# Low parts of weights by adding DMAs at the stage boundaries of a four-layer network, and a later place in the code for the second layer's modulation

## The chip, the cores and the metric

The kernel runs on 1 core of one Trainium2 chip. The metric is the device time of one execution in microseconds (us); lower is better. A core has five engines that work side by side, each in its own fixed order: TensorE (PE, with its weight loads PEld), VectorE (DVE), ScalarE (ACT), GpSimd (POOL) and SyncE (SP, which here only issues DMAs). ACT and POOL can issue DMAs too.

## What is computed

One sequence of 512 tokens (and 256 context tokens) of width 1024 passes four transformer layers. The first two belong to a diffusion block: differential attention, then neighbourhood attention, each followed by an MLP, with scales and shifts ("modulation") that are made from a condition vector. The last two mix retention and windowed attention and have an MLP too. Cut to the part that the change touches:

```python
h = modulate(rms_norm(x, norm2_g[i]), mod_l[3], mod_l[4])
x = x + mod_l[5] * (jnp.square(jax.nn.relu(h @ w_mlp1[i])) @ w_mlp2[i])      # layers 0 and 1
ff = jnp.square(jax.nn.relu(u @ w_ff1[l])) @ w_ff2[l]                         # layers 2 and 3
mod = jax.nn.silu(c) @ w_mod[i] + b_mod[i]                                    # per layer 0 and 1
```

All in float32. Token counts differ: 512 + 256 columns in layer 0, 512 in layer 1, 528 in layers 2 and 3.

## The kernel before, in words

Activations lie with features on the 128 partitions and tokens in the free dimension. PE multiplies in a faster 32-bit format that keeps fewer bits, so every operand is split: a high part (the value rounded to that format) and a low part (value minus high part). Each product is then three matmuls: high x high, high x low, low x high (`mm3`, line 228).

Every weight tile of 128 x 1024 (512 KB) comes through a ring that `wring` makes: SP loads it into a raw buffer `wr`, ACT copies it to `wh` (the high part), and `parts` computes `wl = wr - wh` by a subtraction (line 250) on POOL, or on DVE where the ring was made with `eng=V`. A ring has a few raw buffers (2 or 3) and 5 to 8 pairs of `wh` and `wl`; a pair comes free when PE has used it, a raw buffer when both readers have.

Stages follow each other: `layer0` (attention), `post(0)` (the output weights `wo`, a norm, the MLP), `layer1`, `post(1)`, then twice `block2` (retention, windowed attention, a mixing product `wmix`, the MLP) with `front` for the first projections of the next one. `mlp` runs over eight blocks c = 0..7 of the hidden width. A block takes four tiles of the first weight and four of the second. In c = 0 and c = 7 the tokens go in two groups one after the other, so that the norm of one group can run while PE works on the other; c = 1..6 take all tokens together, and in all but layer 0 use a scheme with seven instead of eight products, for which `load.sums` adds quarters of the weight tile on POOL. By "boundary" the text means such a c = 0 or c = 7 with the norm, `wo`, `wmix` or `front` beside it.

A norm (`rstd`) squares eight tiles on ACT into `nt`, adds them on DVE into `na`, lets PE sum over the partitions (line 380, tile `n`), takes logarithm and exponential on ACT (`nr`), and then DVE scales (`nt`), ACT writes the high part `bigB` and DVE the low part `bigC`. In an MLP block ACT writes relu into `ms`, DVE squares it (line 884 or 212), ACT makes the high part `hh` and DVE the low part `hl`.

The second layer's modulation (`modulation(1, c)`, six parts) is a chain: SP loads a weight tile `wmg` (one buffer), POOL multiplies it by the condition (line 341, tile `wmu`, one buffer), ACT sums it up.

A scheduler puts the instructions of each engine in order from a simulated time line, so an instruction's place in the code is only its rank; each engine then keeps that order and waits at every instruction until its inputs are there.

Of the kernel before, what the change touches and what calls it, by code (L numbers as in the profile page):

```python
# [10 lines left out]
F32 = mybir.dt.float32  # L11
F32R = mybir.dt.float32r
BF16 = mybir.dt.bfloat16
AF = mybir.ActivationFunctionType
ALU = mybir.AluOpType
# [159 lines left out]
class Program:  # L175
# [59 lines left out]
    def wring(self, *parts, size=1024, low=None, eng=None):  # L235


        ws = [(pl, n) for pl, n, _ in parts for _ in range(n)]
        rs = [(pl, n) for pl, _, n in parts for _ in range(n)]
        aw, ar = count(), count()  # L240

        def raw():
            w, n = rs[next(ar) % len(rs)]
            return self.tl(w, "wr", [128, size], n)

        def parts(r, c, eng):
            w, n = ws[next(aw) % len(ws)]
            h, l = (self.tl(q, tag, [128, size], n, F32R) for q, tag in ((w, "wh"), (low or w, "wl")))
            self.act(h[:, c], r[:, c], AF.Copy)
            eng.tensor_tensor(l[:, c], r[:, c], h[:, c].bitcast(F32), op=ALU.subtract)  # L250
            return h, l

        def load(src, c=slice(0, size)):

            r = raw()
            self.nc.sync.dma_start(r[:, c], src)
            return parts(r, c, eng or self.G)

        def sums(src):

            r, s = raw(), raw()
            self.nc.sync.dma_start(r, src)
            (a11, a12, a22, a21), (s1, s2, s3, s4) = ([t[:, i * 256:i * 256 + 256] for i in range(4)] for t in (r, s))
            for o, a, b, op in ((s1, a21, a22, ALU.add), (s2, s1, a11, ALU.subtract),
                                (s3, a11, a21, ALU.subtract), (s4, a12, s2, ALU.subtract)):
                self.G.tensor_tensor(o, a, b, op=op)
            return parts(r, slice(0, 768), self.G), parts(s, slice(0, 1024), self.V)
        load.sums = sums
        return load
# [171 lines left out]
    def layer0(self):  # L441
        nc, V, T, ap = self.nc, self.V, self.T, self.ap
# [3 lines left out]
        st = ExitStack()  # L446
        with st:
            wp = st.enter_context(self.phase("l0w"))
            load = self.wring((wp, 5, 2), size=768)
            rp = st.enter_context(self.phase("l0r"))  # L450

            def weights(h, u):
# [133 lines left out]
            low = count()  # L586
# [132 lines left out]
    def post(self, i):  # L719
        nc, V, T, ap = self.nc, self.V, self.T, self.ap  # L720
        both = i == 0
        A, B, C = self.Af, self.B, self.C

        if both:
            gs = [(A[:, :, :512], B[:, :, :512], C[:, :, :512], slice(0, 512), 0),
                  (self.af, self.b[:, :, :], self.c[:, :, :], slice(512, 768), 1)]
            joint = gs
        else:
            gs = [(A[:, :, s], B[:, :, s], C[:, :, s], s, 0) for s in (slice(16, 272), slice(272, 528))]
            s = slice(16, 528)  # L730
            joint = [(A[:, :, s], B[:, :, s], C[:, :, s], s, 0)]
        width = 768 if both else 528
        with self.psum(a=(1, 6), n=(1, 2)), self.phase("pw") as wp, self.phase("post") as pl:
            load = self.wring((wp, 8, 2), eng=V) if both else self.wring((self.wp, 5, 2), (wp, 3, 1))
            self.nw, self.nb = (512, 3) if both else (336, 5)
            if not both:
                nc.scalar.dma_start(A[:, :, :16], ap["metaT"])
            for X, H, L, _, j in joint:
                for h in range(EARLY, 8):
                    self.split(H[:, h], L[:, h], X[:, h])  # L740

            cut = [slice(EARLY * 128 if m < EARLY else 0, 1024) for m in range(8)]
            order = (6, 7, 0, 1, 2, 3, 4, 5)
            us = {m: load(ap["wo"][i, m][:, cut[m]], cut[m]) for m in order}
            gate = self.modT[i][:, 2]
            for g, (X, H, L, s, j) in enumerate(gs):
                n = s.stop - s.start
                for m in order:
                    early = m < EARLY
                    o = X[:, m]  # L750
                    if early:
                        xo = o
                    else:
                        xo = self.tl(pl, "ms", [128, width], 2)[:, :512 if j == 0 else 256]
                        nc.scalar.dma_start(xo, (ap["xT"], ap["ctxT"])[j][:, m] if both else self.spill[:, m])
                    p = self.pt("a")[:, :n]
                    wh, wl = us[m]
                    self.mm3([p], [(wh[:, k * 128:(k + 1) * 128], wl[:, k * 128:(k + 1) * 128],
                                    [H[:, k]], [L[:, k]]) for k in range(EARLY if early else 0, 8)])
                    if not both and not early:  # L760
                        xo = xo.rearrange("p (c r) -> p r c", r=8)[:, 4 * g:4 * g + 4]
                        p = p.rearrange("p (r c) -> p r c", r=4)
                        o = o.rearrange("p (r c) -> p r c", r=4)
                    V.scalar_tensor_tensor(o, p, gate[:, m, j:j + 1], xo, op0=ALU.mult, op1=ALU.add)
                self.norm_mod(pl, i, 3, X, n, j, H, L)

            gate5 = self.modT[i][:, 5]

            def fin(m, c, g, p):
                X, j = g[0], g[4]  # L770
                V.scalar_tensor_tensor(X[:, m], p, gate5[:, m, j:j + 1], X[:, m], op0=ALU.mult, op1=ALU.add)  # L771

            def after(g):
                X, H, L, s, j = gs[g]
                if both:
                    self.norm_mod(pl, 1, 0, X, s.stop - s.start, j, H, L)
                else:
                    self.b2_norm(pl, 0, g)
                    if g == 1 and self.stop > 1:
                        self.front(0)  # L780

            if both:
                for c in (1, 0, 2, 3, 4, 5):
                    self.modulation(1, c)
            else:
                self.decays(pl)
            fast = None
            if not both:
                fast = [g[3] for g in gs], [self.split4(t) for t in (self.tl(self.b5, "bigD", [128, 8, 528], 1, F32R), self.F)]
            self.mlp(pl, load, ap["w1"][i], ap["w2"][i], width, (gs, joint, gs), fin, after, fast)  # L790

    def mlp(self, pl, load, w1, w2, width, gs, fin, after, fast=None, before=None):

        V, G, T = self.V, self.G, self.T

        def block(us, j, k):

# [86 lines left out]
        for c in range(8):  # L887
            quick = fast and 0 < c < 7
            if c == 7 and before:
                before()  # L890
            u1 = [(load.sums if quick else load)(w1[c * 4 + j]) for j in range(4)]
            u2 = [load(w2[c * 4 + j]) for j in range(4)]
            hid = [(self.tl(pl, "hh", [128, width], 4, F32R), self.tl(pl, "hl", [128, width], 4, F32R))
                   for j in range(4)]
            parts = [gs[1]] if 0 < c < 7 else [[g] for g in gs[c // 7 * 2]]
            if quick:
                for j in range(0, 4, 2):
                    product7(u1[j:j + 2], hid[j:j + 2])
            for i, part in enumerate(parts):
                if not quick:  # L900
                    for j in range(4):
                        first(u1, j, part, hid[j])
                for m in range(8):
                    second(m, c, u2, part, hid)
                if c == 7:
                    after(i)
            if fast and c == 0:
                sums()


    def layer1(self):
        nc, V, T, G, ap = self.nc, self.V, self.T, self.G, self.ap
        st = ExitStack()
        with st:
            st.enter_context(self.psum(pj=(1, 2), tq=(1, 1), s=(1, 2), n=(1, 2), po=(1, 1)))

            pp, wp, kp, lp, pl = (st.enter_context(self.phase('l1' + n)) for n in 'pwkla')
            load = self.wring((wp, 5, 2), size=768, low=lp)
            half = (slice(0, 64), slice(64, 128))
            hL, hC = (self.B, self.C), (self.b, self.c)  # L920
            self.spill = self.dr.tile([128, 8, 512], F32, name="spill")
# [160 lines left out]
    def front(self, li):  # L1082
# [6 lines left out]
        QG = (slice(q0, EG[0].stop), EG[1])  # L1089
        QJ = EG if li == 0 else (qa,)  # L1090
        half = (slice(0, 64), slice(64, 128))
        load = self.wring((self.wp, 5, 2))

        def mmu(w, gs, hold=()):
            ps = [self.pt("a")[:, :s.stop - s.start] for s in gs]
# [12 lines left out]
        class Rot:  # L1108
# [3 lines left out]
                u.f, u.keys = f, keys  # L1112
                u.groups, u.joint = (EG, EG) if keys else (QG, QJ)

            def start(u):
                u.w = load(ap["wfm"][li, u.f])
                u.raw = self.tl(self.b5, "rr", [128, 528], 2)

            def run(u, gs):
# [51 lines left out]
        class Gate:  # L1171
# [2 lines left out]
            def __init__(u, h):  # L1174
                u.h = h

            def start(u):
                u.w = load(ap["wfm"][li, 8 + u.h])
                u.raw = self.tl(self.b5, "gr", [128, 528], 2)

            def run(u, gs):
# [8 lines left out]
        Gate.groups, Gate.joint = QG, QJ  # L1190
        units = [(("k", 0), Rot(4, True)), (("q", 0), Rot(0, False)), (("g", 0), Gate(0)), (("g", 1), Gate(1))]
        for _, u in units:
            u.start()
            u.run(u.groups[:1])
        self.parts = lows, units, load, mmu, Rot, Gate, score, gate, qa, QG, QJ, half

# [408 lines left out]
```

## Time and profile before

| | |
|---|---|
| median of 3 runs | 3781.81 us (3781.76 to 3787.19) |
| the profiled execution | 3784.63 us |
| its span (first to last instruction) | 3782.8 us |
| mean granted TensorE clock | 0.963 of full speed |
| busy share PE, DVE, ACT, POOL | 92%, 67%, 50%, 48% |

PE is the busiest engine, but the table is an average: in long stretches of the MLPs PE is busy all the time, and at the boundaries it waits for what DVE and ACT make. A change at the boundaries is to be read there.

### The profile page before, as it was taken

To read this page: it belongs to the slowest core of one execution; us is meant where nothing else is said; L and a number is where in the kernel's file an instruction comes from. 1 tells how busy PE (TensorE), PEld (TensorE's weight loads), DVE (VectorE), ACT (ScalarE), POOL (GpSimd) and SP (SyncE) were. 2 spreads that over 40 slices of the span, in tenths; PEclk is the share of its full clock that TensorE was granted. 3 is DMA by queue.
4 is the path that set the end of the run, shared out by engine and by line. 5 is a ranking of instruction groups with operands and counts; after the bars stand their busy time and mean duration, and the time that the engine had idled before them with its cause. 6 is when DMAs were issued, how large, how long until landed. Compare 5 with 4: busy or idle time off the path is not lost.

```text
span 3782.8 us, 58120 instructions
## 1 busy us (share of the span) xinstructions
PE 3484.6 (92%) x22512; PEld 3186.7 (84%) x22512; DVE 2529.1 (67%) x4189; ACT 1887.8 (50%) x3891; POOL 1816.3 (48%) x1218
## 2 busy tenths in 40 slices
PE   6888887999999999899999999979997999988998
PEld 6788876878888998788899999979997888787888
DVE  5778867543335777777677666486667767558766
ACT  5777766432125876533356665443334666544333
POOL 4666654430002655587732332457763233356884
PEclk9999998999999999899999999989999999999999
DMA  5222223432112222223332221323332222242333
GB/s 197 78 73 70 67 95 124 151 117 73 56 56 73 58 61 67 81 84 101 112 100 77 78 73 55 112 74 102 93 127 84 82 88 73 61 133 64 101 95 106
DMA packets 118566, 338.00 MB, mean 89 GB/s; under 512 B 13905, under 2 KB 37330, under 8 KB 118034
## 3 DMA queue, kind: packets, MB, share of 16 engines
q1 hardware_dynamic: 105664, 315.97, 26.8%
q10 hardware_dynamic: 12626, 18.32, 1.6%
q8 instruction: 176, 2.88, 0.3%
q14 instruction: 100, 0.82, 0.1%
HBM read 321.39 MB, written 12.86 MB: 88 GB/s over the span
## 4 chain that ended last, share of the span: by engine, by line
PE 54%; DVE 22%; ACT 7%; issue 6%; DMA 5%; POOL 5%; ACTq 0%; POOLq 0%; SPq 0%; DVEq 0%
PE a L228 40%; PE pj L228 6%; DMA wmg<-in_wmod 3%; DVE ms L884 3%; POOL wmu L341 3%; DVE hl L217 2%; DVE P L649 1%; DVE ms L212 1%; ACT wh L207 1%; DVE na L212 1%; DVE nt L212 1%; POOL wl L250 1%; PE po L1307 1%; DVE bigC L217 1%; ACT qd L207 1%
## 5 line engine op out<-in xcount | busy, mean ns | idle before, releaser
L250 POOL TENSOR_TENSOR wl<-wr,wh 128x1024 fp32r<-128x1024 f32 (+2 forms) x416 | 971.4, 2347 | 1032.5 <-ACT wh L207 913.5
L207 ACT ACTIVATE wh<-wr 128x1024 fp32r<-128x1024 f32 (+3 forms) x560 | 536.9, 972 | 758.9 <-PE a L228 409.4
L228 PE MATMUL a<-bigB,wh 128*128 128x256 f32 (+3 forms) x2140 | 637.0, 315 | 25.8 <-ACT bigB L216 16.3
L228 PE MATMUL a<-bigC,wh 128*128 128x256 f32 (+3 forms) x2140 | 643.7, 315 | 9.6 <-DVE bigC L217 9.6
L228 PE MATMUL a<-bigB,wl 128*128 128x256 f32 (+3 forms) x2140 | 640.0, 314 | 1.4 <-DVE wl L250 1.4
L228 PE MATMUL a<-hl,wh 128*128 128x256 f32 (+2 forms) x1664 | 492.9, 334 | 19.0 <-DVE hl L217 18.6
L228 PE MATMUL a<-hh,wh 128*128 128x256 f32 (+2 forms) x1664 | 465.8, 333 | 36.7 <-ACT hh L216 25.5
L228 PE MATMUL a<-hh,wl 128*128 128x256 f32 (+2 forms) x1664 | 486.8, 331 | 0.0
L341 POOL TENSOR_TENSOR wmu<-wmg,sc 128x1024 f32<-128x1024 f32 x128 | 320.7, 2505 | 271.9 <-DMA wmg<-in_wmod 190.5
L228 PEld LDWEIGHTS a<-bigB,wh 128*128 128x128 f32 x2140 | 395.6, 192 | 53.3 <-ACT bigB L216 18.2
L228 PEld LDWEIGHTS a<-bigC,wh 128*128 128x128 f32 x2140 | 396.5, 191 | 37.4 <-DVE bigC L217 13.9
L228 PEld LDWEIGHTS a<-bigB,wl 128*128 128x128 f32 x2140 | 396.2, 191 | 25.5 <-DVE wl L250 2.1
L228 PEld LDWEIGHTS a<-hh,wh 128*128 128x128 f32 x1664 | 288.3, 193 | 75.2 <-ACT hh L216 30.1
L228 PEld LDWEIGHTS a<-hl,wh 128*128 128x128 f32 x1664 | 296.8, 193 | 61.2 <-DVE hl L217 33.6
L250 DVE TENSOR_TENSOR wl<-wr,wh 128x1024 fp32r<-128x1024 f32 (+1 forms) x144 | 203.9, 1423 | 180.3 <-ACT wh L207 180.3
L228 PEld LDWEIGHTS a<-hh,wl 128*128 128x128 f32 x1664 | 295.8, 193 | 26.5
L228 PE MATMUL a<-bigF,wh 128*128 128x256 f32 (+3 forms) x1024 | 295.1, 294 | 4.1 <-ACT bigF L216 4.1
L217 DVE TENSOR_TENSOR hl<-ms,hh 128x512 fp32r<-128x512 f32 (+4 forms) x160 | 198.7, 1261 | 61.4 <-ACT hh L216 60.6
L228 PEld LDWEIGHTS a<-bigF,wh 128*128 128x128 f32 x1024 | 194.2, 192 | 7.2 <-ACT bigF L216 4.6
L209 ACT ACTIVATE wmu<-wmu 128x1024 f32<-128x1024 f32 x128 | 135.1, 1056 | 118.2 <-POOL wmu L341 117.7
L228 PE MATMUL a<-bigD,wh 128*128 128x256 f32 (+2 forms) x640 | 187.0, 303 | 5.8 <-ACT bigD L216 3.3
L771 DVE SCALAR_TENSOR_TENSOR bigA<-a,modT,bigA 128x512 f32<-128x512 f32 (+1 forms) x144 | 96.2, 687 | 140.3 <-PE a L228 140.2
(350 smaller groups left out, 8711.8 us busy)
## 6 DMA issues: line engine op xcount, KB each, us to landing
wr<-in_w SPq DMA_DIRECT2D x128, 512.0 KB, 3.6
wr<-in_wf SPq DMA_DIRECT2D x128, 512.0 KB, 3.5
wmg<-in_wmod SPq DMA_DIRECT2D x80, 512.0 KB, 3.5
wr<-in_wfm SPq DMA_DIRECT2D x76, 512.0 KB, 3.5
wr<-in_wqkv SPq DMA_DIRECT2D x64, 384.0 KB, 3.3
wm<-in_wmod SPq DMA_DIRECT2D x16, 512.0 KB, 7.5
wr<-in_wv SPq DMA_DIRECT2D x16, 512.0 KB, 3.4
wr<-in_wret SPq DMA_DIRECT2D x16, 512.0 KB, 3.5
```

Source lines behind the costliest of these rows:

```text
L207: self.S.activation(o, i, f, bias=bias, scale=scale)
L209: self.S.activation(o, i, f, bias=bias, scale=scale, accum_out=accum)
L212: self.V.tensor_tensor(o, a, b, op=op)
L217: self.V.tensor_tensor(lo, src, hi.bitcast(F32), op=ALU.subtract)
L228: self.T.matmul(o, w, x, start=(i == 0 and j == 0), stop=(i == n - 1 and j == 2))
L250: eng.tensor_tensor(l[:, c], r[:, c], h[:, c].bitcast(F32), op=ALU.subtract)
L341: self.G.tensor_tensor(u, w, self.sc[:, j], op=ALU.mult)
L649: V.scalar_tensor_tensor(P[0], P[1], cf[:, t:t + 1], P[0], op0=ALU.mult, op1=ALU.add)
L771: V.scalar_tensor_tensor(X[:, m], p, gate5[:, m, j:j + 1], X[:, m], op0=ALU.mult, op1=ALU.add)
L884: V.scalar_tensor_tensor(r[:, s], r[:, s], 0.0, r[:, s], op0=ALU.max, op1=ALU.mult)
L1307: T.matmul(po[g], x[:n, t - 1], y[:, s], start=False, stop=(t == 4 and j == 2))
```

## The change

Where a `load` gets `eng=None`, the low part is now made without a subtraction: ACT writes minus the high part into `wl`, and a DMA issued by POOL adds the weight from DRAM to it (`accum_op=ALU.add`). This path is taken by the `wo` tiles of both `post`s, the `wmix` tiles, all eight tiles of blocks c = 0 and c = 7 of the four MLPs, and the first four units of `front`: 104 tiles, 12 of them of 128 x 256. Of these, 80 were subtractions on POOL and 24 on DVE. Blocks c = 1..6 keep their engine, and so do the attention stages. The call of `modulation(1, c)` moves from ahead of the MLP of layer 0 to behind its blocks 1 to 6.

```diff
-        def parts(r, c, eng):
+        def parts(r, c, eng, src=None):
             self.act(h[:, c], r[:, c], AF.Copy)
-            eng.tensor_tensor(l[:, c], r[:, c], h[:, c].bitcast(F32), op=ALU.subtract)
+            if eng is None:
+                self.act(l[:, c], h[:, c].bitcast(F32), AF.Copy, scale=-1.0)
+                self.G.dma_start(l[:, c], src, accum_op=ALU.add)
+            else:
+                eng.tensor_tensor(l[:, c], r[:, c], h[:, c].bitcast(F32), op=ALU.subtract)
...
-            load = self.wring((wp, 8, 2), eng=V) if both else self.wring((self.wp, 5, 2), (wp, 3, 1))
+            load = self.wring((wp, 8, 2)) if both else self.wring((self.wp, 5, 2), (wp, 3, 1))
...
-            if both:
-                for c in (1, 0, 2, 3, 4, 5):
-                    self.modulation(1, c)
-            else:
+            if not both:
                 self.decays(pl)
...
+            self.mlp(pl, load, ap["w1"][i], ap["w2"][i], width, (gs, joint, gs), fin, after, fast,
+                     beside=(lambda c: self.modulation(1, (1, 0, 2, 3, 4, 5)[c])) if both else None)
...
+        eng = G if fast else V, None
...
-            u1 = [(load.sums if quick else load)(w1[c * 4 + j]) for j in range(4)]
-            u2 = [load(w2[c * 4 + j]) for j in range(4)]
+            if quick:
+                u1 = [load.sums(w1[c * 4 + j]) for j in range(4)]
+            else:
+                u1 = [load(w1[c * 4 + j], eng=eng[c in (0, 7)]) for j in range(4)]
+            u2 = [load(w2[c * 4 + j], eng=eng[c in (0, 7)]) for j in range(4)]
...
+            if beside and 0 < c < 7:
+                beside(c - 1)
```

Three places of the resulting order. First POOL at the start of `post(0)`, where before only the modulation of layer 1 (`wmu`) stood, first before and then after the change:

```order
L341 TENSOR_TENSOR wmu_5792<-wmg_5790,sc 128x1024
L341 TENSOR_TENSOR wmu_5795<-wmg_5790,sc 128x1024
L341 TENSOR_TENSOR wmu_5800<-wmg_5798,sc 128x1024
L341 TENSOR_TENSOR wmu_5803<-wmg_5798,sc 128x1024
L341 TENSOR_TENSOR wmu_5808<-wmg_5806,sc 128x1024
```

```order
L345 TENSOR_TENSOR wmu_7336<-wmg_7334,sc 128x1024
L345 TENSOR_TENSOR wmu_7339<-wmg_7334,sc 128x1024
L252 DMA wl_5317<-in_wo 128x1024
L345 TENSOR_TENSOR wmu_7344<-wmg_7342,sc 128x1024
L252 DMA wl_5324<-in_wo 128x1024
L252 DMA wl_5331<-in_wo 128x256
L252 DMA wl_5338<-in_wo 128x256
L345 TENSOR_TENSOR wmu_7347<-wmg_7342,sc 128x1024
L252 DMA wl_5345<-in_wo 128x256
```

The modulation stands at the same place among POOL's instructions although its call moved: the first adding DMA of `wo` comes behind the sixth `wmu` of the second part, and the second one behind the seventh.

Second, PE at the boundary into the MLP of `block2(0)`: the last products of `wmix` (`bigD`, `bigF` their operands) and the sum `n` of the first token group's norm, before and after:

```order
L228 MATMUL a_25161<-bigD_18834,wl_24659 128x256
L228 MATMUL a_25161<-bigD_18834,wh_24658 128x256
L228 MATMUL a_25161<-bigF,wh_24658 128x256
L228 MATMUL a_25161<-bigD_18834,wl_24659 128x256
L380 MATMUL n_24944<-na_24945,ones 128x272
L228 MATMUL a_25161<-bigD_18834,wh_24658 128x256
L228 MATMUL a_25161<-bigF,wh_24658 128x256
L228 MATMUL a_25161<-bigD_18834,wl_24659 128x256
```

```order
L228 MATMUL a_25247<-bigF,wh_24723 128x256
L228 MATMUL a_25247<-bigD_18886,wl_24724 128x256
L228 MATMUL a_25247<-bigD_18886,wh_24723 128x256
L228 MATMUL a_25247<-bigF,wh_24723 128x256
L384 MATMUL n_25004<-na_25005,ones 128x272
L228 MATMUL a_25247<-bigD_18886,wl_24724 128x256
L228 MATMUL a_25468<-bigB,wh_25406 128x272
L228 MATMUL a_25498<-bigB,wh_25406 128x272
```

Before, `n` stands behind 15 of the 24 matmuls of the last product but one; 33 more of `wmix` follow it, and then the MLP's first product, which takes `bigB`, the result of that norm. Now `n` stands one matmul ahead of that first product, 32 places later than before.

Third, ACT at the same boundary, around the norm of the first token group (`nt` the squares, `nr` its logarithm and exponential, `bigA` copies out of PSUM, `bigB` high parts), before and after:

```order
L207 ACTIVATE wh_25370<-wr_25368 128x1024
L207 ACTIVATE bigA_72<-a_25109 128x256
L207 ACTIVATE nt_24965<-bigA_72 128x272
L207 ACTIVATE wh_25376<-wr_25374 128x1024
L207 ACTIVATE bigA_72<-a_25135 128x256
L207 ACTIVATE nr_24969<-n_24944,eps 128x272
L207 ACTIVATE na_25214<-bigA_72 128x256
L207 ACTIVATE nr_24969<-nr_24969 128x272
```

```order
L207 ACTIVATE wl_25435<-wh_25434 128x1024
L207 ACTIVATE wh_25441<-wr_25439 128x1024
L207 ACTIVATE bigA_72<-a_25195 128x256
L207 ACTIVATE nt_25025<-bigA_72 128x272
L207 ACTIVATE wl_25442<-wh_25441 128x1024
L207 ACTIVATE wh_25448<-wr_25446 128x1024
L207 ACTIVATE bigA_72<-a_25221 128x256
L207 ACTIVATE wl_25449<-wh_25448 128x1024
L207 ACTIVATE wh_25455<-wr_25453 128x1024
L207 ACTIVATE nr_25029<-n_25004,eps 128x272
L207 ACTIVATE na_25274<-bigA_72 128x256
L207 ACTIVATE nr_25029<-nr_25029 128x272
```

The last square now stands one product's copy (`bigA`) later, three `wh` copies and the `wl` negations of the second weight stand ahead of the logarithm, and a fourth negation, which the excerpt's end leaves out, stands between logarithm and exponential (with one more copy out of PSUM).

## Rows read from the trace of the kernel before

**Rows 1.** The page: span, and busy time of each engine.

```profile
span 3782.8 us, 58120 instructions
PE 3484.6 (92%) x22512; PEld 3186.7 (84%) x22512; DVE 2529.1 (67%) x4189; ACT 1887.8 (50%) x3891; POOL 1816.3 (48%) x1218
```

**Rows 2.** Table by stretch: length, busy PE, PEld, DVE, ACT, POOL, clock, DMA, GB/s.

```profile
560.00:670.00 110.00, 82.96 (x370) 65.78 (x371) 84.71 (x97) 64.42 (x117) 46.09 (x20) 0.89 0.40 129
830.00:1120.00 290.00, 290.00 (x1651) 252.61 (x1651) 112.48 (x139) 63.76 (x84) 6.30 (x9) 1.00 0.19 59
1530.00:1670.00 140.00, 120.63 (x811) 113.15 (x812) 111.80 (x172) 63.86 (x127) 98.73 (x74) 0.88 0.28 89
...
2450.00:2610.00 160.00, 138.38 (x1024) 134.34 (x1023) 128.51 (x206) 64.83 (x125) 104.25 (x74) 0.91 0.31 94
...
2790.00:2940.00 150.00, 124.13 (x939) 120.25 (x939) 105.44 (x182) 65.40 (x131) 60.99 (x41) 0.92 0.33 106
3370.00:3500.00 130.00, 105.60 (x754) 98.35 (x753) 110.62 (x181) 54.55 (x114) 82.51 (x60) 0.93 0.29 91
```

**Rows 3.** The page's groups of weight splitting: count, busy us, mean ns, idle before.

```profile
L250 POOL TENSOR_TENSOR wl<-wr,wh 128x1024 fp32r<-128x1024 f32 (+2 forms) x416 | 971.4, 2347 | 1032.5 <-ACT wh L207 913.5
L207 ACT ACTIVATE wh<-wr 128x1024 fp32r<-128x1024 f32 (+3 forms) x560 | 536.9, 972 | 758.9 <-PE a L228 409.4
...
L250 DVE TENSOR_TENSOR wl<-wr,wh 128x1024 fp32r<-128x1024 f32 (+1 forms) x144 | 203.9, 1423 | 180.3 <-ACT wh L207 180.3
```

**Rows 4.** Timeline of DVE, 2449 to 2472 us: start, duration, instruction, count.

```profile
2455.77 0.98 DVE L212 TENSOR_TENSOR na<-na,nt 128x272 f32<-128x272 f32 x2
2457.60 2.11 DVE L212 TENSOR_TENSOR bigA<-nt,xo 128x272 f32<-128x272 f32 x1 [0.86 <-DMA xo<-spill]
...
2460.34 6.01 DVE L212 TENSOR_TENSOR na<-na,nt 128x272 f32<-128x272 f32 x4
...
2471.32 2.41 DVE L217 TENSOR_TENSOR bigC<-nt,bigB 128x272 fp32r<-128x272 f32 x1 [0.31 <-ACT bigB L216]
```

**Rows 5.** Timeline of POOL in the same stretch.

```profile
2456.99 2.43 POOL L250 TENSOR_TENSOR wl<-wr,wh 128x1024 fp32r<-128x1024 f32 x1 [2.15 <-ACT wh L207]
2461.20 4.85 POOL L250 TENSOR_TENSOR wl<-wr,wh 128x1024 fp32r<-128x1024 f32 x2 [1.79 <-ACT wh L207]
```

**Rows 6.** Timelines of PE, then of ACT, at the same boundary.

```profile
2466.40 1.28 PE L380 MATMUL n<-na,ones 128*128 128x272 f32 x2 [7.39 <-DVE na L212]
2473.59 0.67 PE L228 MATMUL a<-bigB,wh 128*128 128x272 f32 x4
...
2470.86 1.70 ACT L216 ACTIVATE bigB<-nt 128x272 fp32r<-128x272 f32 x5
```

**Rows 7.** Waits of PE for `na`, 1530 to 1670, then 3370 to 3500 us: total, times, longest.

```profile
PE n L380 <- DVE na L212: 3.6, 1, 3.6
...
PE n L380 <- DVE na L212: 8.1, 2, 7.2
```

**Rows 8.** Waits of PE, 1900 to 1990 us.

```profile
PE a L228 <- DVE hl L217: 4.4, 2, 3.8
```

**Rows 9.** Waits of PE, 2790 to 2940 us.

```profile
PE n L380 <- DVE na L212: 9.9, 1, 9.9
...
PE a L228 <- DVE bigC L217: 2.7, 2, 2.3
PE a L228 <- DVE hl L217: 2.6, 2, 1.5
```

**Rows 10.** DMA issues of 512 KB, by tile: count, KB each, median us to landing.

```profile
wr<-in_wf SPq DMA_DIRECT2D x128, 512.0 KB, 3.5
...
wm<-in_wmod SPq DMA_DIRECT2D x16, 512.0 KB, 7.5
```

**Rows 11.** Timeline from 566 us: POOL's modulation products, PE's first use of a low part.

```profile
567.30 2.36 POOL L341 TENSOR_TENSOR wmu<-wmg,sc 128x1024 f32<-128x1024 f32 x1 [1.26 <-ACT wmu L209]
570.79 0.79 PE L228 MATMUL a<-bigB,wl 128*128 128x512 f32 x1 [1.35 <-DVE wl L250]
575.82 2.40 POOL L341 TENSOR_TENSOR wmu<-wmg,sc 128x1024 f32<-128x1024 f32 x1 [6.16 <-DMA wmg<-in_wmod]
```

More of the change, by code (lines that the diff above doesn't have):

```diff
@@ L249, in parts, with load @@
             self.act(h[:, c], r[:, c], AF.Copy)
-            eng.tensor_tensor(l[:, c], r[:, c], h[:, c].bitcast(F32), op=ALU.subtract)
+            if eng is None:
[3 more added lines that the diff above has]
+                eng.tensor_tensor(l[:, c], r[:, c], h[:, c].bitcast(F32), op=ALU.subtract)
             return h, l
-        def load(src, c=slice(0, size)):
+        def load(src, c=slice(0, size), eng=eng):
             r = raw()
             self.nc.sync.dma_start(r[:, c], src)
-            return parts(r, c, eng or self.G)
+            return parts(r, c, eng, src)
         def sums(src):
@@ L448, in layer0 @@
             wp = st.enter_context(self.phase("l0w"))
-            load = self.wring((wp, 5, 2), size=768)
+            load = self.wring((wp, 5, 2), size=768, eng=self.G)
             rp = st.enter_context(self.phase("l0r"))
@@ L789, in post, with mlp @@
                 fast = [g[3] for g in gs], [self.split4(t) for t in (self.tl(self.b5, "bigD", [128, 8, 528], 1, F32R), self.F)]
-            self.mlp(pl, load, ap["w1"][i], ap["w2"][i], width, (gs, joint, gs), fin, after, fast)
-    def mlp(self, pl, load, w1, w2, width, gs, fin, after, fast=None, before=None):
+            self.mlp(pl, load, ap["w1"][i], ap["w2"][i], width, (gs, joint, gs), fin, after, fast,
+                     beside=(lambda c: self.modulation(1, (1, 0, 2, 3, 4, 5)[c])) if both else None)
+    def mlp(self, pl, load, w1, w2, width, gs, fin, after, fast=None, before=None, beside=None):
         V, G, T = self.V, self.G, self.T
+        eng = G if fast else V, None
         def block(us, j, k):
@@ L917, in layer1 @@
             pp, wp, kp, lp, pl = (st.enter_context(self.phase('l1' + n)) for n in 'pwkla')
-            load = self.wring((wp, 5, 2), size=768, low=lp)
+            load = self.wring((wp, 5, 2), size=768, low=lp, eng=G)
             half = (slice(0, 64), slice(64, 128))
@@ L1091, in front @@
         half = (slice(0, 64), slice(64, 128))
-        load = self.wring((self.wp, 5, 2))
+        G = self.G
+        load = self.wring((self.wp, 5, 2), eng=G)
         def mmu(w, gs, hold=()):
@@ L1113, in __init__, with start @@
                 u.groups, u.joint = (EG, EG) if keys else (QG, QJ)
-            def start(u):
-                u.w = load(ap["wfm"][li, u.f])
+            def start(u, eng=G):
+                u.w = load(ap["wfm"][li, u.f], eng=eng)
                 u.raw = self.tl(self.b5, "rr", [128, 528], 2)
@@ L1175, in __init__, with start @@
                 u.h = h
-            def start(u):
-                u.w = load(ap["wfm"][li, 8 + u.h])
+            def start(u, eng=G):
+                u.w = load(ap["wfm"][li, 8 + u.h], eng=eng)
                 u.raw = self.tl(self.b5, "gr", [128, 528], 2)
@@ L1192, in front @@
         for _, u in units:
-            u.start()
+            u.start(None)
             u.run(u.groups[:1])
```

## The prediction

> **What bounds the kernel now.** I read the page's busy shares first: PE is busy 92% of the span, some 298 us are left over [rows 1]. A table by stretch says where those lie: between 830 and 1120 us, inside the MLP of layer 0, PE is busy for all of its 290 us at the full clock, while in the stretches at the boundaries it idles 16 to 27 us each and the granted clock falls to 0.88 to 0.93 [rows 2]. There DVE is busy about 80% of the time, and POOL works beside it. So PE bounds the inside of the MLPs, where no edit can win, and the chain through DVE and ACT bounds the boundaries; all that the change does is to be priced at the boundaries.
>
> What lengthens that chain is seen by laying DVE's timeline against POOL's at one boundary. Two adds `na` of 128x272 take 0.98 us while POOL is idle, so 0.49 each; four of them take 6.01 us across two POOL subtractions of 4.85 us in all; one `bigA` of the same size takes 2.11 us where it meets a POOL subtraction of 2.43, and `bigC` takes 2.41 [rows 4, 5]. A DVE operation with two SBUF inputs is thus held until POOL's subtraction ends. On the path into `n` this costs 6.01 - 4x0.49 = 4.0 and 2.11 - 0.49 = 1.6 us, together 5.7, and there PE waits 7.4 us [rows 6]. The same wait is 3.6 and 7.2 us at the two like boundaries [rows 7].
>
> **The change part by part.** It takes 80 subtractions from POOL, 80 x 2.347 = 188 us, and 24 from DVE, 24 x 1.423 = 34 us. It gives ACT 104 negations of up to 0.972 us, at most 101 us [rows 3], 104 DMA issues to POOL, and 92 x 512 KB + 12 x 128 KB = 49.6 MB of weights that are read a second time. In the boundary stretches DMA is busy 0.28 to 0.40 [rows 2].
>
> The trace has no POOL issue of an adding DMA and no landing of one. Issue: from 0 to 2.35 us (the subtraction that it replaces); I take 1, as it moves no data itself. Landing: the two transfers of 512 KB shown take 3.5 and 7.5 us [rows 10]; I take 5, nearer to the weights' 3.5 since the source is a weight too, with more for reading the destination. A low part thus comes 0.97 + 1 + 5 = 7.0 us after its high part, where POOL's came 2.35 after: 4.6 us later, between 2.1 (0 and 3.5) and 8.5 (2.35 and 7.5).
>
> The Trainium skill, "DMA: Bandwidth & Descriptors", section "Anatomy of one DMA", fits a POOL-issued DMA as 2.0 us plus the bytes by 436 GB/s; an estimate from it is 3.2 us for 512 KB, and with that term (d) below would be about half. It speaks of plain transfers, and no run here shows an adding one.
>
> (a) *Three boundaries from `wo` or `wmix` into c = 0* (1530, 2450, 3370 us). At 2450 PE was ready for `n` at 2466.40 - 7.39 = 2459.01. In the new order `n` stands 32 matmuls later; one takes 138.38/1024 = 0.135 us [rows 2], so PE reaches it at 2459.0 + 4.3 = 2463.3. Freed of POOL, `na` is done at 2466.4 - 5.7 = 2460.7; two more ACT operations on the way to the last square (a negation and a `wh` copy, 0.97 each) make it 2462.6. So `n` waits for nothing and runs at 2463.3. But its 33 matmuls of cover have gone ahead of it, and behind it PE now waits for `bigB`. Before, `n` started at 2466.40 and the first of five `bigB` was there at 2470.86 + 0.34 [rows 6], 4.8 us later; with the negation that now stands between logarithm and exponential, 5.8. First product: 2469.1 instead of 2473.59, a gain of 4.5. The old wait of 7.4 is replaced by one of some 4.5 (5.8 less `n` itself at 1.28) behind `n`. I take 4.5 for the boundary at 3370 too, and 2 at 1530, where only 3.6 was to be had: **-11**. If all of ACT's five inserted operations fell on the chain, at 0.97 each, nothing would be left of it: bounds -16 to 0.
>
> (b) *The c = 7 stretches and the end.* PE waits 4.4 us for `hl` at 1900 [rows 8], 2.7 for `bigC` and 2.6 for `hl` at 2790 [rows 9]; both are subtractions of DVE with two SBUF inputs, beside POOL's. Half of this, 4.9, and 1 at the end of the kernel: **-6**. The 9.9 us for `na` at 2790 I leave: the norm there waits for its own chain. Bounds -11 to 0.
>
> (c) *`post(0)`*. DVE loses 34 us of subtractions in an MLP where PE idles 110 - 83 = 27 us in the first stretch alone [rows 2]; most of the 34 lies beside products, a fifth counts: -7. Against it, POOL's in-order queue: the first adding DMA stands behind the sixth `wmu`, which ended at 567.30 + 2.36 = 569.7. It lands at 569.7 + 1 + 5 = 575.7, while PE used that low part at 570.79 [rows 11]: +5. The second stands behind the seventh, which ends at 578.2, and lands at 584.2; the first tile's 24 matmuls, at 82.96/370 = 0.22 us each [rows 2], last 5.4 of the 8.5 us between them; the rest falls among products of the context tokens that can be taken meanwhile or not. With that left at nothing, **-2**; bounds -20 to +8. The modulation moved in the code but not in POOL's order, and I cost that at nothing: its products run in POOL's gaps, as before.
>
> (d) *Later low parts.* 4.6 us more per tile are hidden where the ring runs ahead. It holds eight pairs, and a tile lasts PE 24 x 0.135 = 3.2 us per token group, so some 16 us even if only five pairs are ahead; of that 3.5 go to the load, 1 to the copy and 2 to negation and issue, and a landing up to about 9 us stays hidden. What isn't hidden is a first low part at a boundary: +1 at each of six, **+6**; bounds 0 (3.5 us) to +25 (7.5 us, with POOL's issue at 2.35).
>
> (e) *The clock.* At 1.2 or 2.4 GHz, a mean of 0.88 to 0.93 costs 12.1 + 16.8 + 14.4 + 12 + 9.1 = 64 us in the five boundary stretches of the table (length times what is lacking from 1.00); in 830 to 1120, with no idle PE, nothing [rows 2]. The idle of the same stretches sums to 27 + 19 + 22 + 26 + 24 = 118 us. If the two fall together, (a) to (d), some 13 us less idle, return 13/118 x 64 = 7: **-7**; bounds 0 to -14.
>
> The sum: -11 - 6 - 2 + 6 - 7 = -20. The profiled execution took 3784.6 us, so 3764.6; that one stands 2.8 above the median, so about **3762** on the medians' scale.
>
> **The rivals.**
> *All of the lock comes back* (18%). DVE's operations are held not only in the waits I counted but all along the boundaries; with POOL free for some 60 to 100 us of each stretch, PE idle could halve: 118/2 = 59 with a share of the clock, less the lateness of (d) and (c), some 45: 3715 to 3747, middle 3737. For it: POOL was busy 61 to 104 us in four of the five stretches, mostly with such subtractions. Against: in many of those waits ACT ends last, and ACT's work grows.
>
> *ACT takes it back: no change* (16%). 101 us of negations lie in ACT's order among squares, logarithms and copies out of PSUM. ACT is busy only 40 to 50% at the boundaries, but its place in the chain counts: two more operations than I counted in each of seven boundaries are 14 us, and the gain with its clock is gone: 3774 to 3789.
>
> *The low parts come too late: slower* (22%). The mechanism is (d) with a longer landing L. From about 9 us on, each further us falls on PE, at the seven boundaries at once, and in `post(0)` the first wait grows by the full L - 5. At L = 14 this is 7 x 5 + 9 = 44 us against the gain of 20: 3806. For it: the 7.5 us of one kind of transfer, and ACT and POOL which hand a tile on in order. Against: DMA is two thirds idle at the boundaries. In the extreme the landing sets the pace: a block c = 0 uses eight tiles in 8 x 2 x 3.2 = 52 us, 6.5 each; at 7.5 one after another it would take 8 us longer in seven blocks, +56, and 3820 with the other terms. The Trainium skill, "Collectives: The Full Stack", section "The bandwidth ceiling", has a reduction at half the rate of a copy, since it reads two sources for each chunk and not since it adds; no run here shows this. By that, the estimate for a tile would go from 3.2 to some 4.4 us, which is not beyond 6.5.
>
> *The modulation isn't moved in fact*: the order shows it, and it gives no time of its own.
>
> **How the numbers follow.** Main case 44%, 3747 to 3774; larger gain 18%; same 16%; slower 22%, of which 6 lie beyond 3810. About 0.2%, 7.6 us, is what a measurement of this kernel can tell from no change: 3774 to 3789. So faster 62%, same 16%, slower 22%. The range 3728 to 3804 leaves out some 6% below and 12% above. The main case's own range, from half of each bound of (a) to (e) or so, is 3747 to 3774.
>
> **What the changed profile would show.** Right: `na`, `bigA`, `bigC` of 128x272 at 0.43 to 0.49 us at 2450; no wait of PE at `n` there, one of 4 to 6 us for `bigB` behind it; POOL's busy time down by 188 us less its issues, ACT's up by about 100; a landing of `wl` of 3.5 to 7.5 us; PE's first wait in `post(0)` for a low part of 4 to 6 us, put down to a DMA. Wrong: waits of PE for a DMA into `wl` at the boundaries (then the landing is too long), waits for ACT that add up to more than those for DVE fell (then ACT took it back), or a granted clock that stays below 0.93 in the boundary stretches though the waits are gone.

## The result and the profile after

The changed kernel takes 3820.34 us in the median (3814.51 to 3822.52, 4 runs), before beside it 3784.5 us: a ratio of 1.0092, 95% interval 1.008 to 1.0104. It is slower by some 35 us, where 22 us less were forecast, and it lies above the stated range. The profiled execution's page has the span and the busy time of the engines, as [rows 1]:

```profile
span 3812.7 us, 58335 instructions
PE 3474.4 (91%) x22512; PEld 3178.6 (83%) x22512; DVE 2409.8 (63%) x4165; ACT 1976.9 (52%) x3995; POOL 1702.4 (45%) x1242
```

DVE lost 119 us and POOL 114, and ACT gained 89, as planned. PE runs the same number of matmuls in 10 us less of busy time, so its idle time grew by 40 us, from 298 to 338: new waits. The table by stretch answers to [rows 2] (length, busy PE, PEld, DVE, ACT, POOL, clock, DMA share, GB/s). PE comes later to each place now, so a stretch holds a little other work than before:

```profile
560.00:670.00 110.00, 74.52 (x319) 58.69 (x319) 46.55 (x67) 69.61 (x121) 52.82 (x34) 0.82 0.66 174
830.00:1120.00 290.00, 289.04 (x1645) 251.73 (x1644) 107.84 (x137) 68.59 (x91) 8.64 (x8) 1.00 0.25 71
1530.00:1670.00 140.00, 107.87 (x781) 102.26 (x782) 97.56 (x170) 75.22 (x146) 70.89 (x64) 0.89 0.48 125
2450.00:2610.00 160.00, 132.94 (x997) 127.83 (x996) 111.18 (x199) 70.32 (x135) 74.51 (x67) 0.91 0.40 110
2790.00:2940.00 150.00, 131.76 (x1019) 129.06 (x1018) 88.66 (x170) 70.83 (x127) 47.81 (x46) 0.93 0.56 155
3370.00:3500.00 130.00, 106.84 (x793) 103.79 (x794) 82.77 (x162) 59.48 (x126) 49.50 (x50) 0.88 0.51 134
```

The inside of the MLP is untouched. At all five boundaries DVE has more room, and the DMA share has risen: 0.40 to 0.66 in the first stretch, 0.28 to 0.48 in the third. At 560, 1530 and 2450 PE is nonetheless less busy, by 5 to 13 us; at 3370 it is about as busy as before, and at 2790, a c = 7 with `front`, busier by 7.6 us.

DVE's timeline at the boundary of [rows 4] shows that the lock is gone and what came in its place:

```profile
2470.18 0.44 DVE L212 TENSOR_TENSOR bigA<-nt,xo 128x272 f32<-128x272 f32 x1 [3.32 <-DMA xo<-spill]
...
2472.99 0.44 DVE L212 TENSOR_TENSOR bigA<-nt,xo 128x272 f32<-128x272 f32 x1 [1.43 <-DMA xo<-spill]
2475.98 0.44 DVE L212 TENSOR_TENSOR bigA<-nt,xo 128x272 f32<-128x272 f32 x1 [2.54 <-DMA xo<-spill]
...
2477.81 0.44 DVE L212 TENSOR_TENSOR bigA<-nt,xo 128x272 f32<-128x272 f32 x1 [1.04 <-DMA xo<-spill]
2478.16 2.07 DVE L212 TENSOR_TENSOR na<-na,nt 128x272 f32<-128x272 f32 x4
2483.15 0.44 DVE L212 TENSOR_TENSOR bigA<-nt,xo 128x272 f32<-128x272 f32 x1 [2.91 <-DMA xo<-spill]
```

Four `na` take 2.07 us where they took 6.01, but DVE now waits five times, 11.2 us in all, for `xo`, the residual that SP loads back. These two of PE's waits in 2450 to 2610 (total, times, longest) answer to [rows 6]:

```profile
PE a L228 <- ACT bigB L216: 7.3, 2, 5.3
PE n L384 <- DVE na L212: 5.1, 1, 5.1
```

PE waits at `n` again, 5.1 us for 7.4, and then 5.3 behind it for `bigB`, which the new order had uncovered. ACT waits for no weight here: between `n` and `bigB` it works on its own copies and negations. The DMA issues (KB each, median us to landing) tell why `xo` is late; those of before and of after:

```profile
xo<-spill SPq DMA_DIRECT2D x24, 128.0 KB, 3.0
```

```profile
wl<-in_wf POOLq DMA_DIRECT2D x32, 512.0 KB, 8.9
...
wl<-in_wmix POOLq DMA_DIRECT2D x16, 512.0 KB, 11.1
...
xo<-spill SPq DMA_DIRECT2D x24, 128.0 KB, 6.7
```

The adding DMAs land after 9 to 11 us, not 5, and the `xo` loads beside them take twice as long. The third cost is at the start of `wmix`, first on ACT's timeline and then on PE's:

```profile
2427.98 2.94 ACT L207 ACTIVATE wl<-wh 128x1024 fp32r<-128x1024 f32 x3
...
2431.14 2.94 ACT L207 ACTIVATE wh<-wr 128x1024 fp32r<-128x1024 f32 x3
```

```profile
2432.24 0.59 PE L228 MATMUL a<-bigD,wh 128*128 128x272 f32 x1 [4.19 <-ACT wh L207]
2432.63 0.43 PE L228 MATMUL a<-bigF,wh 128*128 128x272 f32 x1
2436.70 0.60 PE L228 MATMUL a<-bigD,wl 128*128 128x272 f32 x1 [3.64 <-DMA wl<-in_wmix]
```

Three `wh` copies wait behind three negations on ACT, and the first low part then lands 3.6 us too late: 7.8 us where the longest wait for `wh` was 0.4 before. PE's order puts no other product there.

### The profile page after: what moved, and what is told of

Its sections match the earlier page's. It is cut to its first block, busy times and chain, and to the rows that moved or that the text cites. A ratio compares the mean times of both kernels' runs of the same rounds, so it can differ in the third digit from the quotient of the medians.

```text
span 3812.7 us, 58335 instructions
## 1 busy us (share of the span) xinstructions
PE 3474.4 (91%) x22512; PEld 3178.6 (83%) x22512; DVE 2409.8 (63%) x4165; ACT 1976.9 (52%) x3995; POOL 1702.4 (45%) x1242
## 3 DMA queue, kind: packets, MB, share of 16 engines
q0 software_dynamic: 14976, 49.81, 7.1%
## 4 chain that ended last, share of the span: by engine, by line
PE 57%; DVE 18%; DMA 8%; ACT 8%; issue 5%; POOL 4%; ACTq 0%; SPq 0%; POOLq 0%; DVEq 0%
PE a L228 43%; PE pj L228 6%; DMA wmg<-in_wmod 3%; POOL wmu L345 3%; DVE ms L888 2%; DVE P L653 1%; DVE hl L217 1%; ACT wh L207 1%; PE po L1317 1%; DVE ms L212 1%; ACT qd L207 1%; DMA xo<-spill 1%; PE po L1062 1%; DMA wr<-in_wo 1%; DVE nt L212 1%
## 5 line engine op out<-in xcount | busy, mean ns | idle before, releaser
L254 POOL TENSOR_TENSOR wl<-wr,wh 128x1024 fp32r<-128x1024 f32 (+1 forms) x336 | 766.3, 2291 | 838.3 <-ACT wh L207 721.7
L228 PE MATMUL a<-bigB,wh 128*128 128x256 f32 (+3 forms) x2140 | 641.1, 317 | 52.1 <-ACT bigB L216 42.1
L254 DVE TENSOR_TENSOR wl<-wr,wh 128x1024 fp32r<-128x1024 f32 x120 | 173.6, 1452 | 165.9 <-ACT wh L207 165.8
L217 DVE TENSOR_TENSOR hl<-ms,hh 128x512 fp32r<-128x512 f32 (+4 forms) x160 | 186.9, 1186 | 64.7 <-ACT hh L216 64.0
L228 PE MATMUL a<-bigD,wl 128*128 128x256 f32 (+2 forms) x640 | 185.1, 300 | 7.5 <-DMA wl<-in_wmix 7.5
```

What stands on the lines that cost most here:

```text
L217: self.V.tensor_tensor(lo, src, hi.bitcast(F32), op=ALU.subtract)
L228: self.T.matmul(o, w, x, start=(i == 0 and j == 0), stop=(i == n - 1 and j == 2))
```

## The experiments

The theory after the result: the adding DMAs land so late, and slow SP's loads so much, that what DVE gains is lost again, most of all where a stage starts. The rival: ACT's negations cost the time, wherever they stand. The first four kernels each make one part of the change alone. In all ratios the denominator is the kernel before, on the same chip.

**Modulation alone.** The diff's `beside=` part, all low parts as before.

> Only the later call of the second layer's modulation; all low parts as before. Theory (the adding DMAs and ACT's negations cost the time): no change, within 4 us of before. Rival (the modulation's products and sums, moved in the planner's order, cost it): +8 us or more, with longer waits of PE for bigB in post(0).

Measured 1.0000 (0.9992 to 1.0009): no change.

**c = 7 alone.**

```diff
-                u1 = [load(w1[c * 4 + j], eng=eng[c in (0, 7)]) for j in range(4)]
+                u1 = [load(w1[c * 4 + j], eng=eng[c in (7,)]) for j in range(4)]
```

and the same for `u2`; `wo`, `wmix`, `front` and the modulation as before.

> Adding DMAs only in blocks c = 7 (32 tiles), modulation called as before. Theory (a low part that lands 8 us late costs only where its tile is needed at once, and c = 7 has its tiles loaded ahead): faster, -8 to -14 us, from the waits for hl and bigC at 1900 to 1990 and 2790 to 2940. Rival (ACT's negations cost wherever they stand): +5 us, or no change.

Measured 1.0015 (1.0006 to 1.0024), some 6 us slower: a miss for the theory, and the rival's number. PE's waits from 1900 to 1990 show why nothing was gained:

```profile
PE a L228 <- DVE hl L217: 4.4, 2, 3.8
```

That is the row of [rows 8] unchanged. The subtractions that hold DVE there are those of `front`'s units, which this kernel left on POOL, not those of c = 7. What was lost shows elsewhere: in the whole run PE waits 6.9 us for low parts that a DMA brings, 3.4 of them at the end of the kernel; before there was no such wait.

**c = 0 alone.** The same edit with `(0,)`.

> Adding DMAs only in blocks c = 0 (32 tiles), modulation called as before. Theory: relief of DVE and new waits (bigB behind ACT's negations, xo loads that land late beside the adding DMAs) about cancel, +2 to +12 us, most of it in the two post stages. Rival (ACT's negations cost everywhere alike): +5 us here and in the runs with c = 7 alone and with the projections alone.

Measured 1.0010 (1.0001 to 1.0019), +4 us: gain and loss about cancel, which fits the theory's numbers and the rival's alike.

**`wo`, `wmix` and `front` alone.** The edit with `()`.

> Adding DMAs only for wo, wmix and the first units of front, modulation called as before. Theory (the first low parts of a stage have no cover: wh copies behind negations 4 us, wl landing 3.5 to 5 us at each of the four wo and wmix stages): slower, +20 to +30 us. Rival (negations cost everywhere alike): +6 us.

Measured 1.0042 (1.0028 to 1.0056), +16 us: more than the rival's 6 and less than the theory's 20.

**`front` alone.** As the last, and both rings of `wo` and `wmix` get their engine back:

```diff
-            load = self.wring((wp, 8, 2)) if both else self.wring((self.wp, 5, 2), (wp, 3, 1))
+            load = self.wring((wp, 8, 2), eng=self.V) if both else self.wring((self.wp, 5, 2), (wp, 3, 1), eng=self.G)
...
-            load = self.wring((self.wp, 5, 2), (wp, 3, 1))
+            load = self.wring((self.wp, 5, 2), (wp, 3, 1), eng=self.G)
```

> Adding DMAs only for the first four units of front (two times 4 tiles); wo, wmix and the MLPs as before, modulation called as before. Theory (front's subtractions on POOL are what holds DVE at 1900 to 1990 and 2790 to 2940, and their tiles are needed late): faster, -10 to -18 us, as the gains of 8 us at 1930 and 9 us at 2860 to 2940 in the run with the projections alone. Rival (those gains are only earlier delays that the next wait swallowed): 0 to -4 us.

Measured 0.9967 (0.9955 to 0.998): 12 us faster than before. No wait of PE for `hl` is left in 1900 to 1990. By difference to the run before, `wo` and `wmix` cost 0.75%, 28 us, by themselves. The five parts sum to 0.0 + 0.15 + 0.10 + 0.75 - 0.33 = 0.67%; the whole has 0.92%. The 0.25% between them, some 9 us, would arise only when the parts run together, but it is hardly larger than the intervals of the runs summed.

**Negations on DVE.**

```diff
-                self.act(l[:, c], h[:, c].bitcast(F32), AF.Copy, scale=-1.0)
+                self.V.tensor_scalar(l[:, c], h[:, c].bitcast(F32), -1.0, None, op0=ALU.mult)
```

> The changed kernel with the negations on DVE instead of ACT, adding DMAs as they are. Theory that ACT's order makes half of the loss (negations ahead of the norm's logarithm and exponential, wh copies behind negations at the start of wo and wmix): 12 to 20 us below the changed kernel, 0.4 to 0.6% above before. Rival (the landing of the adding DMAs makes nearly all of it): within 5 us of the changed kernel.

Measured 1.0046 (1.0032 to 1.006): with the adding DMAs in place, taking the negations off ACT returns about half of the loss, 17 us; the other half stays. PE's waits for `bigB` in the whole run fall from 42.1 to 23.6 us.

**Negations without a DMA.**

```diff
-                self.G.dma_start(l[:, c], src, accum_op=ALU.add)
+                self.G.tensor_tensor(l[:, c], r[:, c], h[:, c].bitcast(F32), op=ALU.subtract)
```

> The changed kernel with the negations on ACT left in, but POOL's subtraction writes over them in place of each adding DMA (104 tiles, POOL also where DVE subtracted before). Theory that ACT's order makes half of the loss: +12 to +20 us against before, with DVE held by POOL again. Rival (the landing makes nearly all): +0 to +6 us.

Measured 1.0034 (1.0022 to 1.0047), +13 us, inside the first theory's numbers. The 13 us hold ACT's negations together with 24 subtractions that moved from DVE to POOL.

**Without the residual load `xo`**, in the kernel before and in that with c = 0 alone. Both leave a term out of the result; each is compared with the kernel before, timed beside them.

```diff
-                    xo = self.tl(pl, "xo", [128, 272], 3)[:, :n]
-                    nc.sync.dma_start(xo, spill[:, m, s])
...
-                    self.tt(A[:, m, s], t, xo, ALU.add)
+                    self.tt(A[:, m, s], t, A[:, m, s], ALU.add)
```

> The kernel before, but the residual after wmix isn't loaded back (xo): the add takes its own input twice in place of it, so the stream that it should add is left out. The yardstick for the next run. Both theories: 0 to -5 us against before.

Measured 1.0007 (0.9998 to 1.0015): no gain.

> Adding DMAs only in blocks c = 0, and the same residual left out. Theory that xo loads landing late beside the adding DMAs ate the gain at the two wmix boundaries: PE's waits for na there (4.0 and 5.6 us with c = 0 alone) fall under 1 us, and the difference to the kernel before without xo is -4 to -10 us. Rival (the norm's chain on ACT ate it): the waits for bigB grow by what the waits for na lose, and the difference stays at +4 us.

Measured 1.0012 (1.0003 to 1.0022), so +2 us against the kernel before without `xo`, with intervals that overlap. At 2450 the wait for `na` went, as the theory had it, but the time did not: the wait moved on to `bigB` (11.4 us), as the rival had it. ACT's timeline at this boundary shows what stood behind it, which neither had named, and SP's the issues that belong to it:

```profile
2466.35 0.47 ACT L207 ACTIVATE nr<-n,eps 128x272 f32<-128x272 f32 x1
2466.72 0.41 ACT L207 ACTIVATE na<-bigA 128x256 f32<-128x256 f32 x1
2474.31 1.06 ACT L207 ACTIVATE wh<-wr 128x1024 fp32r<-128x1024 f32 x1 [7.18 <-DMA wr<-in_wf]
2475.27 0.36 ACT L207 ACTIVATE bigA<-a 128x256 f32<-128x256 f32 x1
2475.54 0.42 ACT L207 ACTIVATE nr<-nr 128x272 f32<-128x272 f32 x1
```

```profile
2457.12 0.63 SPq L1403 DMA_DIRECT2D spill<-bigA  x1
2458.04 4.10 SPq L260 DMA_DIRECT2D wr<-in_wf  x2
```

A `wh` copy stands between the norm's logarithm and its exponential, and ACT, in order, waits 7.2 us for the weight of that copy. SP had issued that load at 2458.04, right behind a store of 1 MB (`spill`); it takes some 16 us to 2474.31, where a 512 KB load has a median of 3.5 [rows 10]. From 2440 to 2470 the loads of `wr` in this kernel land so (us, min, median, max, of those whose landing is on the trace), and in the kernel before from 2420 to 2470:

```profile
DMA to landing us min/median/max: 3.4/10.9/16.3
```

```profile
DMA to landing us min/median/max: 3.5/4.3/6.2
```

So the DMAs that POOL issues delay the high parts too, not only the low ones. In the kernel before, the loads behind the same store land after 4.8 to 6.2 us, so the store alone doesn't do it. The same row of the changed kernel (2425 to 2490), and then of the kernel with plain loads in place of the adding ones that follows below (2411 to 2470):

```profile
DMA to landing us min/median/max: 3.5/7.8/12.4
```

```profile
DMA to landing us min/median/max: 3.5/5.6/13.8
```

The median is longer with the add; the longest landing, behind the store in both, is as long without it.

**`front` and c = 0, negations on DVE.** The edits of the runs above together.

> Adding DMAs for front's first units and for blocks c = 0, negations on DVE; wo, wmix, c = 7 and the modulation as before. Theory (the gain of front stays, and c = 0 loses most by ACT's negations in the norm): -11 to -18 us, faster than the run with front alone. Rival (c = 0 loses by the landing): -4 to -8 us.

Measured 0.9946 (0.9933 to 0.9958), 20 us faster than before and the lowest ratio of the study, though its interval overlaps with that of `front` alone, so what c = 0 adds is not clear of the noise, and PE still waits 4.9 us at `n` and 5.0 for `bigB` at the boundary of 2450.

**Plain loads in place of the adding ones.**

```diff
-                self.G.dma_start(l[:, c], src, accum_op=ALU.add)
+                self.G.dma_start(l[:, c], src)
```

> The changed kernel with plain loads in place of the adding ones (the low part is then the weight itself, so the low products are wrong): only the landing is asked for. If the add with its read of the destination makes the 8.5 to 11 us: about 4 us as SP's loads of 512 KB. If it is the queue from POOL: 8 us and more, as with the add.

The low part is then the weight itself, so this kernel multiplies other numbers. One run took 3778.15 us. The landing gave neither answer cleanly: 5.4 to 6.7 us lie between SP's 4 and the 8.5 to 11 of the add. The same kernel over more runs:

> The kernel with plain loads in place of the adding ones once more, now timed (the low products are wrong). Theory that adding, by its slow transfers and what they do to the others, makes nearly all of the 0.9%: 0.996 to 1.000 of before. Rival (ACT's negations make a third or more of it): 1.003 or more.

Measured 0.997 (0.9956 to 0.9984): everything else of the change in place, ACT's negations and the second read of 49.81 MB too, and the kernel is 11 us faster than before. Whether the other numbers change the granted clock was not tested. Its DMA rows, the queue first:

```profile
q0 software_dynamic: 14976, 49.81, 4.1%
...
wl<-in_wf POOLq DMA_DIRECT2D x32, 512.0 KB, 5.8
...
xo<-spill SPq DMA_DIRECT2D x24, 128.0 KB, 3.9
```

and the queue's row of the changed kernel:

```profile
q0 software_dynamic: 14976, 49.81, 7.1%
```

The same packets and bytes take 1.7 times the engines' time with the add. PE's waits from 2440 to 2480 in the kernel with plain loads are these:

```profile
PE a L228 <- ACT bigB L216: 5.9, 1, 5.9
PE a L228 <- DVE bigC L217: 0.3, 1, 0.3
```

No wait at `n`, one for `bigB`: what the prediction had for the changed kernel. At the start of `wmix`, ahead of this, the wait for the `wh` copies is as long as with the add (4.2 us), and the first low part is 1.6 us late, for 3.6 (2400 to 2470):

```profile
PE a L228 <- ACT wh L207: 5.3, 4, 4.2
PE a L228 <- DMA wl<-in_wmix: 1.6, 1, 1.6
```

At 1530 to 1670 the wait for `bigB`, 2.6 us in the kernel before, stays long too; with the add and then with plain loads:

```profile
PE a L228 <- ACT bigB L216: 13.5, 1, 13.5
```

```profile
PE a L228 <- ACT bigB L216: 10.6, 1, 10.6
```

**`wo` (layer 1) and `wmix` subtracted on DVE**, besides `front` and c = 0:

```diff
-            load = self.wring((self.wp, 5, 2), (wp, 3, 1), eng=self.G)
+            load = self.wring((self.wp, 5, 2), (wp, 3, 1), eng=self.V)
```

and the same for the ring of `post(1)`.

> As the run with front and c = 0 and negations on DVE, but the low parts of wo (layer 1) and wmix are subtracted on DVE instead of POOL (24 tiles, 1.2 to 1.4 us each). Theory (POOL's subtractions hold DVE there, and DVE idles while wo and wmix run): a few us below that run, 0.992 to 0.994 of before. Rival (DVE's own time in these stages counts): 0.995 to 0.997.

Measured 0.9952 (0.9941 to 0.9964): not to be told from the run with POOL there; the rival's numbers.

## Why the prediction was wrong

**The step that failed is the landing of the adding DMA, and term (d) that was worked out from it.** The prediction set the landing at 5 us with an upper bound of 7.5, "nearer to the weights' 3.5", and took the other transfers as they were. It took both ends from plain transfers, which hold no bound for one that reads its destination. Measured: 8.5 and 8.9 us in the median for the MLP weights, 11.1 for `wmix`, up to 15.9 among six issued close together; and the neighbours suffered, `xo` from 3.0 to 6.7 us in the median. Taking the add away and nothing else turns 1.0092 into 0.997, that is 1.2% or 46 us (39 to 53 by the two intervals), more than the whole loss.

The longer landing in the prediction's own working is not enough, though. Its rival "the low parts come too late" charges each us beyond 9 at seven boundaries and the full L - 5 in `post(0)`: at 11.1 us that is 15 + 6 = 21 us, which cancels the gain of 20 and gives no change. The rival named the right mechanism, with 3806 at a landing of 14 us, but only its extreme reached 3820. Both put at nothing, without a reason, that one transfer slows another; and the cover that the ring lacks where a stage starts they priced at 1 us a boundary.

**The sum's terms one by one.**

(a) The lock went as worked out (0.44 us for each `na` and `bigA`). With plain loads the boundaries at 2450 and 3370 came out as written, no wait at `n` and 5.9 and 4.9 us for `bigB` against 4 to 6. With the add, `xo` makes `n` late at 2450, and the forecast wait for `bigB` comes on top: 10.4 us of waiting against 7.4. At 1530 the prediction misread its row: the 3.6 us of [rows 7] are those of a later `n`, at 1579.66, and the first group's `n` did not wait. Four negations stand there between logarithm and first `bigB`, not one; from the one to the other ACT needs 13.0 us, where it needed 5.8 (10.1 with plain loads). For -11, c = 0 measured +4 alone.

(b) was booked at the wrong place: the waits for `hl` from 1900 on belong to `front`'s subtractions (c = 7 alone left them, `front` alone removed them). `front` gave -12 and c = 7 cost 6, so that the term of -6 holds for the two together is luck.

(c) PE waits 4.7 us for the first low part of `post(0)`, against +5, which is luck as well: the landing took 7.8 us, but POOL came to its issue at 566.4, not at 569.7. The modulation's new place in the code is worth nothing, as said. The relief of 7 us did not come, since PE waits there 7.8 us for `na` and 12.9 for `bigB`, where it waited 7.4 and 7.6 before.

(d) is the term most out of size: +6 for all tiles, against +28 for `wo` and `wmix` alone (with what (c) has of `wo`). The ring's cover of "some 16 us" is real inside an MLP block, where PE waits 4.8 us in the whole run for 64 such low parts, and missing at a stage's start: for the 32 of `wo` and `wmix` it waits 17.3 us. The prediction applied the cover to both.

(e) The mean granted clock went from 0.963 to 0.961 instead of up. Of 49.6 MB read a second time the queue shows 49.81; nothing rests on that.

**ACT's part.** The rival "ACT takes it back" is half right. Negations on DVE return 17 us, yet with plain loads the same negations on ACT leave the kernel faster than before. That kernel is faster on balance only: it gains 11 us where 22 were forecast, with a landing of 5.4 to 7.1 us, inside the bounds. PE's waits for `bigB` in the whole run, before, with the add and with plain loads, are these:

```profile
PE a L228 <- ACT bigB L216: 16.3, 5, 7.6
```

```profile
PE a L228 <- ACT bigB L216: 42.1, 8, 13.5
```

```profile
PE a L228 <- ACT bigB L216: 36.7, 8, 10.6
```

With plain loads PE waits 17 us less for `na` than before (62.1 to 45.2), but 20 us more for `bigB`: what DVE gives, the norm's chain through ACT takes, though ACT waits for no weight at 1530 or 2450 there. With the add, taking the negations off ACT lowers the waits for `bigB` to 23.6. So ACT's work in its fixed order costs at the norms even while the loads are punctual, and late weights add to it (ACT at 7.2 us behind one weight shows this at one place).

What the add itself brings is seen in other waits too: those for low parts that a DMA brings are 22.1 us with it and 9.5 with plain loads, those for `na` 53.6 and 45.2. How the 46 us divide between late low parts, late high parts, late residuals and the granted clock (0.957 to 0.961 in the runs with the add, 0.962 to 0.966 with plain loads) was not separated by a run.

The range was too narrow on the upper side because (d) was bounded by the longest plain transfer of 512 KB, and because no rival let one transfer slow another.

## What to carry to other kernels

A DMA that adds can free a compute engine, but price it from a transfer of its own kind: here it landed 1.3 to 1.6 times as late as a plain load from the same queue, and over twice as late as SP's loads. Price also what it does to every other load in the same stretch. Use it where its tile is wanted late and where the lock that it removes really lies (here the eight tiles of `front`: 0.9967; with c = 0 and the negations off ACT 0.9946, though the intervals overlap), and not for the first tiles of a stage. In an in-order engine look at which copies stand ahead of a short step on the path, and whether a late load is among them: the wait shows under the short step's name.

## What the runs showed of the hardware

An adding DMA costs POOL 0.86 to 0.88 us to issue in the median, a plain one 0.53. No hold of DVE shows beside it: `na` of 128x272 stays at 0.43 to 0.44 us. Of 128 KB it lands after 7.2 us in the median, of 512 KB after 7.3 to 11.1; plain loads of 512 KB from POOL after 5.4 to 7.1, from SP mostly after 3.5. So the size hardly shows in these medians, all taken beside other traffic. Six issued within 8 us at the start of `wmix` land, with the add and then without:

```profile
DMA to landing us min/median/max: 7.1/12.7/15.9
```

```profile
DMA to landing us min/median/max: 5.0/7.5/8.2
```

The same bytes take 1.7 times the engines' time with the add (7.1% against 4.1%). The Trainium skill says of a reduction between cores, in "Collectives: The Full Stack", section "The bandwidth ceiling", that it runs at about half the rate of a copy because each chunk reads two sources. The trace comes near to it in the queue's time, 1.7 times; that the reading is the reason isn't shown by a run here.
